# A mixture of experts on one core: gate and up products take both exact parts of the tokens as one 512-column operand, and the token search is spread one product a step over a whole expert

## The chip, the cores and the metric

The kernel runs on one core of a Trainium2 chip. The metric is the device time of one execution in microseconds (us), as the median of several runs. A profile of one further execution gives the time of every instruction on every engine: PE (TensorE matrix products), PEld (TensorE weight loads, which overlap PE), DVE (VectorE), ACT (ScalarE), POOL (GpSimd) and SP (SyncE, which issues DMAs). An instruction is named by its line in the kernel, its engine and operation, and output<-inputs by the program's names.

## The reference, cut to what matters

A layer has a mixer (normalisation, gated delta rule in two directions, pooling, output projection) and then a mixture of experts. The change touches the second half only. Of `T = 2048` tokens of width `D = 1024`, each of 16 experts takes the `cap = 256` tokens with the highest router probability.

```python
def _expert_choice_ffn(xn, router_w, w_gate, w_up, w_down):
    cap = EC_CAPACITY * T // N_EXPERTS
    probs = jax.nn.softmax(jnp.einsum('btd,de->bte', xn, router_w).astype(jnp.float32), axis=-1)
    gate, idx = lax.top_k(jnp.swapaxes(probs, 1, 2), cap)
    xg = xn[bidx, idx]
    h = jax.nn.silu(jnp.einsum('becd,edf->becf', xg, w_gate)) * jnp.einsum('becd,edf->becf', xg, w_up)
    y = jnp.einsum('becf,efd->becd', h, w_down) * gate[..., None].astype(xn.dtype)
    return jnp.zeros_like(xn).at[bidx, idx].add(y)
```

The layer's output is `h` plus this sum, normalised once more. `w_gate` and `w_up` are 1024x2048 and `w_down` 2048x1024 per expert, all float32.

## The kernel before, in words

Products are made nearly exact in float32: an operand is split into a part `hi` that the fast float32 format (fp32r) holds and the rest `lo`, and a product is the sum of `hi·hi`, `hi·lo` and `lo·hi`, three matrix products into the same PSUM tile (`split3`, L26 to L32). The stationary operand of a product is a 128x128 block that is loaded first, the moving one has 256 or 512 columns.

The expert stage (`experts`) is a loop over 16 experts, and in it over 8 chunks of 256 columns of `w_gate` and `w_up` (256 rows of `w_down`). `weights` (L1046) loads a chunk (three tiles of 1 MB by SP), ACT copies each into its `hi` part (`hg`, `hu`, `hd`, L1061) and DVE subtracts to get `lo` (`lg`, `lu`, `ld`, L1062). There are two sets of these tiles, so a chunk is prepared while the one before is used. A chunk has two blocks of 128 columns, so an expert has 16 blocks and the stage 256.

A block has three pieces on PE. Gate and up (`gate_up`, L1124): for each, 8 slices of the 1024 rows, and for each slice `split3` with the block of the weights stationary and the token parts `xh` and `xl` (256 columns each) moving, 48 products of 256 columns in all, into the two halves of one PSUM tile `pg`. Then ACT and DVE make the activation from `pg` (L1134 to L1136, the sigmoid by way of a tanh) and split it into `hh` (ACT, L1138) and `hlo` (DVE, L1139). Down (`down`, L1142): 12 products of 512 columns, with `hh` or `hlo` stationary, into four PSUM tiles `y`, which collect over the expert's 16 blocks. The down piece of a block is issued after the gate and up pieces of the next block (`behind`).

The tokens of an expert are found by `topk` (L966): ten steps, each of which compares the probabilities with eight thresholds (DVE, L984), counts (DVE, L988), adds the counts over partitions by one small product `fc` (PE, L990), and picks the next threshold (DVE, L993, L995, L981); then four small products `fr` rank the chosen tokens (L1008, L1009). Each step waits for the one before. It is run for expert 0 ahead of the loop, for expert 1 in the first chunk, and then for five, five and four experts at a time. `tokens` (L1084) turns ranks into row numbers (32 small products `pl`, L1094), `gather` (L1104) fetches the rows (POOL) and transposes them (PE, L1117; ACT and DVE make `xh` and `xl` from PSUM tile `pt`, L1119 and L1120).

What sets the order on an engine: the framework's scheduler puts the instructions of the program into one list per engine, and within a list they run in that order, each waiting for its operands. PSUM has 8 banks: two for `pg`, four for `y`, one for `pt` and one (`pl`) for the search and the row numbers.

Of the kernel before, what the change touches and what calls it, by code (L numbers as in the profile page):

```python
# [14 lines left out]
P = 128  # L15
# [19 lines left out]
class Kernel:  # L35
# [9 lines left out]
    def constants(self, c, mix):  # L45
# [20 lines left out]
        self.mhalf = c.tile([P, 8], F32, name="mhalf")  # L66
# [899 lines left out]
    def topk(self, e0, n, tk, pt, tag, tag0=None):  # L966
# [9 lines left out]
        for r in range(10):  # L976
# [12 lines left out]
            ps = pt.tile([P, n, 8], F32, name="fc", tag=tag if r else tag0 or tag)  # L989
# [29 lines left out]

        ps, rank = ranks(q)  # L1020
# [6 lines left out]
        nc.vector.tensor_tensor(sel[:, 0], rank, q[:, 0], op=OP.add)  # L1027
        _, rank = ranks(sel)
        nc.vector.tensor_tensor(rank, rank, sel[:, 0], op=OP.mult)
        slot = tk.tile([P, n, NT], F32, name="slot", bufs=2)  # L1030
        nc.vector.tensor_scalar(slot, rank, -1.0, None, op0=OP.add)
        return {e0 + k: slot[:, k] for k in range(n)}

    def expert_weights(self, ctx):
# [14 lines left out]
        def weights(e, fc, eng=nc.vector):  # L1049
            W = {}  # L1050
            for nm, w in (("g", wg), ("u", wu), ("d", wd)):
# [7 lines left out]
                o = e // 4 * 4 if nm != "d" else e % 4 * 4  # L1059
                hi, lo = (self.placed(hl, part + nm, sh, o) for part in "hl")  # L1060
# [9 lines left out]
    def experts(self, ctx, dr):  # L1070
# [8 lines left out]
        psg = E(tc.tile_pool(name="psg", bufs=2, reuse_waits="tile", space=bass.MemoryType.PSUM))  # L1079
# [4 lines left out]
        def tokens(e, slot):  # L1084

            oh = self.raw.tile([P, NT, CAP], BF, name="oh", tag="r")
            for n in range(NT):
                nc.vector.tensor_scalar(oh[:, n], self.iota, slot[:, n:n + 1], None, op0=OP.is_equal)
            c = xp.tile([P, 2, 5], F32, name="lc")
            for t in range(2):  # L1090
                ps = pst.tile([P, 5], F32, name="pl")
                for n in range(NT):
                    seg, a = divmod(n, 2)
                    nc.tensor.matmul(ps, oh[:, n, t * P:t * P + P], self.what[:, a, e, seg],  # L1094
                                     start=(n == 0), stop=(n == NT - 1))
                nc.vector.tensor_copy(c[:, t], ps)
# [5 lines left out]
            return idx, gate  # L1102

        def gather(idx, e):  # L1104
            xh, xl = (self.placed(xp, nm, [P, KD, CAP], e % 4 * 4) for nm in ("xh", "xl"))
# [6 lines left out]
            for kp in range(KD // 2):  # L1112
# [8 lines left out]
            return xh, xl  # L1121

        def gate_up(W, f, x, e):

            pg = psg.tile([P, 2, CAP], F32, name="pg")
# [7 lines left out]
            s = hp.tile([P, CAP], F32, name="s", bufs=1)  # L1133
            nc.scalar.activation(s, pg[:, 0], AF.Tanh, scale=0.5)  # L1134
            nc.vector.scalar_tensor_tensor(s, s, 1.0, pg[:, 0], op0=OP.add, op1=OP.mult)
            nc.vector.scalar_tensor_tensor(s, s, 0.5, pg[:, 1], op0=OP.mult, op1=OP.mult)  # L1136
            hh, hl_ = (self.placed(hp, nm, [P, 1, CAP], e // 4 * 4)[:, 0] for nm in ("hh", "hlo"))
# [13 lines left out]
        def scatter(ys, idx, gate):  # L1151
            for t in range(2):
                yo = yp.tile([P, D], F32, name=f"yo{t}")
# [11 lines left out]
        def norm(o, h, sq):  # L1165
# [3 lines left out]
            nc.vector.scalar_tensor_tensor(o, h, ss, tail["w"], op0=OP.mult, op1=OP.mult)  # L1169

        def tail_load(idx):
            w = xp.tile([P, D], F32, name="fnw", tag="xl")
# [3 lines left out]
            hg = xp.tile([P, 2, D], F32, name="hg", tag="xh")  # L1176
# [5 lines left out]
        def tail_rows(j):  # L1182
            h = xp.tile([P, D], F32, name="fh", tag="xg")
            nc.sync.dma_start(h, dr["h"][j * P:j * P + P, :])
            o = yp.tile([P, D], F32, name="fo", tag=f"yo{j % 2}")
            norm(o, h, o)
            nc.sync.dma_start(out2[j * P:j * P + P, :], o)

        def tail_last(ys, idx, gate):
            for t in range(2):  # L1190
                h = tail["h"][:, t]
                for n in range(2):
# [3 lines left out]
                o = yp.tile([P, D], F32, name="fo", tag=f"yo{t}")  # L1196
                norm(o, h, o)
                nc.gpsimd.indirect_dma_start(out=out2, out_offset=bass.IndirectOffsetOnAxis(ap=idx[:, t:t + 1], axis=0),  # L1198
                                             in_=o, in_offset=None)


        slots = self.topk(0, 1, tk, pst, "pl")
        nxt = tokens(0, slots.pop(0))
        xnext = gather(nxt[0], 0)
        behind = None
        for e in range(NE):
            (idx, gate), x = nxt, xnext
            ys = [psy.tile([P, 512], F32, name=f"y{n}") for n in range(4)]
            for fc in range(NF):
                W = first.pop(0) if first else weights(e, fc)  # L1210
                for f in range(FC // P):
                    h = gate_up(W, f, x, e)
                    if behind:
                        behind()
                    ft = fc * (FC // P) + f

                    def behind(e=e, W=W, f=f, h=h, ys=ys, ft=ft, idx=idx, gate=gate):
                        down(W, f, h, ys, ft == 0, ft == FF // P - 1)
                        if ft == FF // P - 1:
                            (scatter if e < NE - 1 else tail_last)(ys, idx, gate)  # L1220
# [81 lines left out]
```

## Time and profile before

| | us |
|---|---|
| median of 3 runs | 3402.22 (3400.2 to 3404.77) |
| profiled execution | 3406.23 |
| its span, first to last instruction | 3404.5 |
| PE busy | 3250.1 (95% of the span) |
| PEld busy | 2939.4 (86%) |
| DVE busy | 2155.9 (63%) |
| ACT busy | 1504.8 (44%) |

The busy time of PE counts each product until its result is written, and successive products overlap, so a busy PE is not yet a PE at its peak: what a product costs in a dense stretch is the time from its start to the next one's start. The first expert's products begin 1165 us into the span and the last ones end at about 3387 us; the clock that the chip grants to PE is full (1.0) through this stage.

### The profile page before, as it was taken

How to read it: one execution, taken by the hardware profiler on the slowest of the kernel's cores; microseconds unless marked ns; L12 is line 12 of the kernel's file. 1: busy time of each engine (PE TensorE's matmuls, PEld its weight loads, DVE VectorE, ACT ScalarE, POOL GpSimd, SP SyncE). 2: the span in 40 equal slices, each digit the busy share in tenths (PEclk: the TensorE clock that was granted, in tenths of full speed). 3: DMA queues.
4: the chain of work that ended last, by engine and by line, in shares of the span. 5: the costliest groups of instructions: out<-in, count | busy, mean ns of one | idle time of the engine just before them, and what ended most of it. 6: DMA issues, size and time to landing. Idle time of an engine off the chain costs nothing. (4 is left out here: it accounts for less than half of the span.)

```text
span 3404.5 us, 54803 instructions
## 1 busy us (share of the span) xinstructions
PE 3250.1 (95%) x21934; PEld 2939.4 (86%) x21934; DVE 2155.9 (63%) x3277; ACT 1504.8 (44%) x2426; POOL 549.3 (16%) x746
## 2 busy tenths in 40 slices
PE   8989989798999499999999999999999999999997
PEld 6877777688888399999999999999999999999997
DVE  7753878666654668665556576665656766656564
ACT  5543663455432244444444444444444444444453
POOL 3531457451121200000000000000000000000012
PEclk9999999899999699999999999999999999999999
DMA  5452444598753546656556575565665656667584
GB/s 158 116 158 84 129 136 122 186 273 265 256 191 118 198 156 210 204 178 219 198 185 211 185 223 198 178 215 182 206 203 179 212 198 186 211 186 223 198 291 148
DMA packets 514383, 644.62 MB, mean 189 GB/s; under 512 B 57168, under 2 KB 413136, under 8 KB 514128
## 3 DMA queue, kind: packets, MB, share of 16 engines
q1 hardware_dynamic: 499856, 597.60, 53.4%
q0 software_dynamic: 9664, 35.13, 4.3%
q10 hardware_dynamic: 4608, 8.39, 0.8%
q8 instruction: 172, 2.82, 0.3%
q14 instruction: 83, 0.68, 0.1%
HBM read 548.23 MB, written 92.02 MB: 188 GB/s over the span
## 5 line engine op out<-in xcount | busy, mean ns | idle before, releaser
L30 PE MATMUL pg<-xh,hg 128*128 128x256 f32 x2048 | 581.1, 284 | 2.5 <-DVE s L1136 1.6
L31 PE MATMUL pg<-xl,hg 128*128 128x256 f32 x2048 | 576.8, 282 | 0.5 <-DVE xl L1120 0.5
L30 PE MATMUL pg<-xh,hu 128*128 128x256 f32 x2048 | 576.4, 281 | 0.0
L32 PE MATMUL pg<-xh,lg 128*128 128x256 f32 x2048 | 576.0, 281 | 0.0
L32 PE MATMUL pg<-xh,lu 128*128 128x256 f32 x2048 | 575.3, 281 | 0.0
L31 PE MATMUL pg<-xl,hu 128*128 128x256 f32 x2048 | 574.2, 280 | 0.0
L1062 DVE TENSOR_TENSOR ld<-rd,hd 128x2048 fp32r<-128x2048 f32 x127 | 291.0, 2291 | 269.9 <-ACT hd L1061 269.7
L30 PEld LDWEIGHTS pg<-xh,hg 128*128 128x128 f32 x2048 | 386.0, 189 | 12.2 <-DVE s L1136 2.7
L31 PEld LDWEIGHTS pg<-xl,hg 128*128 128x128 f32 x2048 | 386.4, 189 | 10.5 <-DVE xl L1120 1.1
L32 PEld LDWEIGHTS pg<-xh,lg 128*128 128x128 f32 x2048 | 386.3, 189 | 1.7
L30 PEld LDWEIGHTS pg<-xh,hu 128*128 128x128 f32 x2048 | 385.8, 188 | 0.1
L31 PEld LDWEIGHTS pg<-xl,hu 128*128 128x128 f32 x2048 | 385.5, 188 | 0.1
L32 PEld LDWEIGHTS pg<-xh,lu 128*128 128x128 f32 x2048 | 385.4, 188 | 0.1
L1148 PE MATMUL y<-hd,hh 128*128 128x512 f32 x1024 | 326.6, 395 | 1.4 <-ACT hh L1138 1.3
L1148 PE MATMUL y<-ld,hh 128*128 128x512 f32 x1024 | 320.6, 394 | 0.0
L1148 PE MATMUL y<-hd,hlo 128*128 128x512 f32 x1024 | 319.4, 394 | 0.0
L1138 ACT CAST hh<-s 128x256 fp32r<-128x256 f32 x256 | 104.0, 406 | 486.9 <-DVE s L1136 486.9
L1062 DVE TENSOR_TENSOR lu<-ru,hu 128x2048 fp32r<-128x2048 f32 x127 | 290.9, 2290 | 42.8 <-ACT hu L1061 42.5
L1061 ACT CAST hd<-rd 128x2048 fp32r<-128x2048 f32 x128 | 243.9, 1905 | 167.4 <-PE y L1148 166.1
L1062 DVE TENSOR_TENSOR lg<-rg,hg 128x2048 fp32r<-128x2048 f32 x127 | 290.9, 2291 | 32.3 <-ACT hg L1061 32.1
L1061 ACT CAST hu<-ru 128x2048 fp32r<-128x2048 f32 x128 | 244.3, 1908 | 99.5 <-PE pg L31 95.6
L1061 ACT CAST hg<-rg 128x2048 fp32r<-128x2048 f32 x128 | 244.3, 1908 | 76.4 <-PE pg L31 72.5
(314 smaller groups left out, 5810.5 us busy)
## 6 DMA issues: line engine op xcount, KB each, us to landing
rg<-in_expert_w_gate_dram SPq DMA_DIRECT2D x128, 1024.0 KB, 6.1
ru<-in_expert_w_up_dram SPq DMA_DIRECT2D x128, 1024.0 KB, 6.1
rd<-in_expert_w_down_dram SPq DMA_DIRECT2D x128, 1024.0 KB, 5.1
wr<-in_w_in_dram SPq DMA_DIRECT2D x40, 512.0 KB, 4.1
xin<-in_x_dram SPq DMA_DIRECT2D x16, 512.0 KB, 4.4
d_P<-pp SPq DMA_DIRECT2D x32, 256.0 KB, 2.3
kT<-d_kT SPq DMA_DIRECT2D x32, 256.0 KB, 4.5
v<-d_v SPq DMA_DIRECT2D x32, 256.0 KB, 4.7
```

The lines of the kernel that those rows point to most:

```text
L30: nc.tensor.matmul(ps, lh, rh, start=first, stop=False)
L31: nc.tensor.matmul(ps, lh, rl, start=False, stop=False)
L32: nc.tensor.matmul(ps, ll, rh, start=False, stop=last)
L1061: nc.scalar.copy(hi, r)
L1062: eng.tensor_tensor(lo, r, hi.bitcast(F32), op=OP.subtract)
L1138: nc.scalar.copy(hh, s)
L1148: nc.tensor.matmul(ys[t * 2 + n], a[:, ts], b[:, f, n * 512:n * 512 + 512], start=st, stop=sp_)
```

## The change

Token parts: `gather` makes one tile `xx` with `xh` and `xl` beside each other, 512 columns per slice. For a slice of gate or up there are now two products: the weights' `hi` against all 512 columns, and the weights' `lo` against the first 256. The first half of the PSUM tile then has `hi·hi`, the second the two cross terms, so each of gate and up has a whole `pg` tile (three bufs), and ACT copies the second half out and DVE adds the first (L1143, L1144) before the activation goes on. A block's gate and up have 32 products and not 48.

Search: `topk` and `tokens` are generators now; each `next` issues the work up to the next small product. The search for expert e+2 runs alone (for experts 1 and 2 together in expert 0), one step per block. The row numbers are sought at blocks 4 and 5 (7 and 8 in expert 0), the rows fetched two blocks after, and the four groups of transposes stand in the last four blocks. Search, row numbers and transposes share one PSUM bank.

Down: for each of the four `y` tiles the three products stand together; before, two tiles took turns. The tiles `yo` and `fo` are gone, results go into `xg` buffers or stay in place, and the weights' tiles start at fixed offsets. Nothing ahead of the expert stage differs but a constant's width (`mhalf`).

```diff
-            ps = pt.tile([P, n, 8], F32, name="fc", tag=tag if r else tag0 or tag)
+            yield
+            ps = pt.tile([P, n, 8], F32, name="fc", tag=tag)
             nc.tensor.matmul(ps, self.onesb, cnt, start=True, stop=True)
...
-        psg = E(tc.tile_pool(name="psg", bufs=2, reuse_waits="tile", space=bass.MemoryType.PSUM))
+        psg = E(tc.tile_pool(name="psg", bufs=3, reuse_waits="tile", space=bass.MemoryType.PSUM))
...
-            c = xp.tile([P, 2, 5], F32, name="lc")
+            yield
+            ps = pst.tile([P, 2, 5], F32, name="pl", tag="pt")
             for t in range(2):
-                ps = pst.tile([P, 5], F32, name="pl")
                 for n in range(NT):
                     seg, a = divmod(n, 2)
-                    nc.tensor.matmul(ps, oh[:, n, t * P:t * P + P], self.what[:, a, e, seg],
+                    nc.tensor.matmul(ps[:, t], oh[:, n, t * P:t * P + P], self.what[:, a, e, seg],
                                      start=(n == 0), stop=(n == NT - 1))
-                nc.vector.tensor_copy(c[:, t], ps)
+            c = xp.tile([P, 2, 5], F32, name="lc")
+            nc.vector.tensor_copy(c, ps)
...
-                oh = xh[:, kp * 2:kp * 2 + 2]
+                oh = xx[:, kp * 2:kp * 2 + 2, 0]
                 nc.scalar.copy(oh, pt)
-                nc.vector.tensor_tensor(xl[:, kp * 2:kp * 2 + 2], pt, oh.bitcast(F32), op=OP.subtract)
+                nc.vector.tensor_tensor(xx[:, kp * 2:kp * 2 + 2, 1], pt, oh.bitcast(F32), op=OP.subtract)
...
-            for half, nm in ((0, "g"), (1, "u")):
+            a = []
+            for nm in ("g", "u"):
                 hi, lo = W[nm]
+                pg = psg.tile([P, 2, CAP], F32, name="pg")
                 for k in range(KD):
-                    split3(nc, pg[:, half], (hi[:, k, fs], lo[:, k, fs]), (x[0][:, k], x[1][:, k]),
-                           k == 0, k == KD - 1)
+                    nc.tensor.matmul(pg, hi[:, k, fs], x[:, k], start=k == 0, stop=False)
+                    nc.tensor.matmul(pg[:, 1], lo[:, k, fs], x[:, k, 0], start=False, stop=k == KD - 1)
+                r = hp.tile([P, CAP], F32, name="r" + nm)
+                nc.scalar.copy(r, pg[:, 1])
+                nc.vector.tensor_tensor(r, pg[:, 0], r, op=OP.add)
+                a.append(r)
...
-                for a, b, st, sp_ in ((h[0], hi, first, False), (h[0], lo, False, False), (h[1], hi, False, last)):
-                    for n in range(2):
+                for n in range(2):
+                    for a, b, st, sp_ in ((h[0], hi, first, False), (h[0], lo, False, False), (h[1], hi, False, last)):
                         nc.tensor.matmul(ys[t * 2 + n], a[:, ts], b[:, f, n * 512:n * 512 + 512],
                                          start=st, stop=sp_)
...
+            if e == 0:
+                search, pace, choose = self.topk(1, 2, tk, pst, "pt", slots), 2, 7
+            else:
+                search, pace, choose = (self.topk(e + 2, 1, tk, pst, "pt", slots) if e + 2 < NE else iter(())), 1, 4
+            listing = iter(())
+            for ft in range(FF // P):
...
+                if ft == choose and e + 1 < NE:
+                    listing = tokens(e + 1, slots.pop(e + 1))
+                h = gate_up(W, f, x)
+                if behind:
+                    behind()
+                for _ in range(pace):
+                    next(search, None)
+                next(listing, None)
+                if e + 1 < NE:
+                    if ft == choose + 2:
+                        xnext, turn = gather(found[e + 1][0])
+                    if ft > last - KD // 2:
+                        turn(ft - last - 1 + KD // 2)
```

How the lists change, first on PE around the start of a down piece in the middle of the stage (`y` tiles by their numbers, `hd` and `ld` the weights' parts, `hh` and `hlo` the stationary ones). Before:

```order
L30 MATMUL pg<-xh,hu 128x256
L31 MATMUL pg<-xl,hu 128x256
L32 MATMUL pg<-xh,lu 128x256
L1148 MATMUL y_15481<-hd,hh 128x512
L1148 MATMUL y_15482<-hd,hh 128x512
L1148 MATMUL y_15481<-ld,hh 128x512
L1148 MATMUL y_15482<-ld,hh 128x512
L1148 MATMUL y_15481<-hd,hlo 128x512
L1148 MATMUL y_15482<-hd,hlo 128x512
```

And now, at the start of another down piece:

```order
L1140 MATMUL pg<-xx,hg 128x512
L1141 MATMUL pg<-xx,lg 128x256
L1163 MATMUL y_17899<-hd,hh 128x512
L991 LDWEIGHTS onesb
L991 MATMUL fc<-fcnt,onesb 128x8
L1163 MATMUL y_17899<-ld,hh 128x512
L1163 MATMUL y_17899<-hd,hlo 128x512
L1163 MATMUL y_17900<-hd,hh 128x512
L1163 MATMUL y_17900<-ld,hh 128x512
L1163 MATMUL y_17900<-hd,hlo 128x512
```

Three products of a slice have become two, the three products of a `y` tile stand together, and a product of a search (`fc`) stands among them. In this row the down piece starts within a gate piece: the scheduler has let the gate piece of a later block begin first.

On DVE, one chunk in the middle of the stage (`ld`, `lg`, `lu` are the splits of the weights, `s` the activation). Before:

```order
L1062 TENSOR_TENSOR ld<-rd,hd 128x2048
L1062 TENSOR_TENSOR lg<-rg,hg 128x2048
L1062 TENSOR_TENSOR lu<-ru,hu 128x2048
L1135 SCALAR_TENSOR_TENSOR s<-s,pg 128x256
L1136 SCALAR_TENSOR_TENSOR s<-s,pg 128x256
L1139 TENSOR_TENSOR hlo<-s,hh 128x256
```

And now, with the adds (`rg`, `ru`) and a step of a search among them:

```order
L994 SCALAR_TENSOR_TENSOR ftot<-fc,fth 128x8
L996 TENSOR_REDUCE fbase<-ftot 128x1
L981 TENSOR_TENSOR fth<-bits,fbase 128x8
L1064 TENSOR_TENSOR ld<-rd,hd 128x2048
L984 TENSOR_TENSOR fge<-fpr,fth 128x128
L1149 SCALAR_TENSOR_TENSOR s<-s,rg 128x256
L1064 TENSOR_TENSOR lu<-ru,hu 128x2048
L1144 TENSOR_TENSOR ru<-pg,ru 128x256
L988 TENSOR_REDUCE fcnt<-fge 128x8
L1150 SCALAR_TENSOR_TENSOR s<-s,ru 128x256
L1144 TENSOR_TENSOR rg<-pg,rg 128x256
L1154 TENSOR_TENSOR hlo<-s,hh 128x256
```

Between a block's second add and its `hlo` there now stand a count of the search and the next block's first add.

## Rows read from the trace of the kernel before

**Rows 1.** The page: busy us, share of the span and instructions of each engine.

```profile
PE 3250.1 (95%) x21934; PEld 2939.4 (86%) x21934; DVE 2155.9 (63%) x3277; ACT 1504.8 (44%) x2426; POOL 549.3 (16%) x746
```

**Rows 2.** Waits on PE from 1190 us: waiting <- waited for: us, times, longest.

```profile
PE pg L30 <- DVE s L1136: 1.6, 2, 1.4
PE y L1148 <- ACT hh L1138: 1.3, 1, 1.3
PE pt L1117 <- DVE xl L1120: 1.0, 1, 1.0
PE pg L31 <- DVE xl L1120: 0.5, 2, 0.3
PE fc L990 <- DVE fcnt L988: 0.2, 1, 0.2
```

**Rows 3.** By window, `pg` alone: length, PE busy (products), granted clock, DMA share, GB/s.

```profile
1455.83:1461.43 5.60, 5.60 (x48) 1.00 0.59 91
1946.14:1951.80 5.66, 5.66 (x48) 1.00 1.06 381
3209.27:3215.08 5.81, 5.81 (x48) 1.00 1.02 362
1500.00:2500.00 1000.00, 685.20 (x5559) 1.00 0.61 197
```

**Rows 4.** The same, products of 512 columns: `y`, then `mm`, then `po`.

```profile
1951.80:1954.58 2.78, 2.78 (x12) 1.00 0.41 129
1500.00:2500.00 1000.00, 342.60 (x1392) 1.00 0.61 197
...
230.39:304.75 74.36, 74.36 (x329) 1.00 0.37 111
...
1081.53:1092.49 10.96, 10.96 (x48) 1.00 0.24 96
```

**Rows 5.** Timeline, PE: start, duration, line, out<-in, count; a search product.

```profile
2007.74 0.39 PE L1148 MATMUL y<-hd,hlo 128*128 128x512 f32 x1
2007.98 0.19 PE L990 MATMUL fc<-fcnt,onesb 128*128 128x40 bf16 x1
2008.01 0.48 PE L1148 MATMUL y<-hd,hlo 128*128 128x512 f32 x1
```

**Rows 6.** Groups of DVE instructions from 1180 us: count, busy us, mean ns, idle before.

```profile
L1139 DVE TENSOR_TENSOR hlo<-s,hh 128x256 fp32r<-128x256 f32 x256 | 108.5, 424 | 93.6 <-ACT hh L1138 92.1
...
L988 DVE TENSOR_REDUCE fcnt<-fge 128x40 bf16<-128x640 bf16 x20 | 16.3, 814 | 0.2
L984 DVE TENSOR_TENSOR fge<-fpr,fth 128x640 bf16<-128x640 f32 x18 | 14.8, 824 | 0.5
...
L984 DVE TENSOR_TENSOR fge<-fpr,fth 128x128 bf16<-128x128 f32 x9 | 2.6, 289 | 0.2
L988 DVE TENSOR_REDUCE fcnt<-fge 128x8 bf16<-128x128 bf16 x9 | 2.5, 281 | 0.1
...
L981 DVE TENSOR_TENSOR fth<-bits,fbase 128x8 int32<-128x8 int32 x9 | 1.5, 164 | 0.2
```

**Rows 7.** Busy time by window: DVE alone, then ACT alone.

```profile
1500.00:2500.00 1000.00, 620.04 (x805) 1.00 0.61 197
...
1500.00:2500.00 1000.00, 431.69 (x434) 1.00 0.61 197
```

**Rows 8.** Timeline of one block: DVE, and the down piece on PE.

```profile
1945.39 2.29 DVE L1062 TENSOR_TENSOR lu<-ru,hu 128x2048 fp32r<-128x2048 f32 x1 [0.49 <-ACT hu L1061]
1947.60 0.41 DVE L1135 SCALAR_TENSOR_TENSOR s<-s,pg 128x256 f32<-128x256 f32 x1
1948.94 0.42 DVE L1139 TENSOR_TENSOR hlo<-s,hh 128x256 fp32r<-128x256 f32 x1 [0.47 <-ACT hh L1138]
...
1952.73 0.62 PE L1148 MATMUL y<-hd,hlo 128*128 128x512 f32 x2
```

**Rows 9.** Timeline, PE: the row numbers of expert 0.

```profile
1150.68 0.57 PE L1094 MATMUL pl<-what,oh 128*128 128x5 bf16 x16 [0.26 <-DVE lc L1096]
```

More of the change, by code (lines that the diff above doesn't have):

```diff
@@ L1027, in topk @@
         nc.vector.tensor_tensor(sel[:, 0], rank, q[:, 0], op=OP.add)
+        yield
         _, rank = ranks(sel)
         nc.vector.tensor_tensor(rank, rank, sel[:, 0], op=OP.mult)
-        slot = tk.tile([P, n, NT], F32, name="slot", bufs=2)
+        slot = tk.tile([P, n, NT], F32, name="slot", bufs=3)
         nc.vector.tensor_scalar(slot, rank, -1.0, None, op0=OP.add)
-        return {e0 + k: slot[:, k] for k in range(n)}
+        slots.update({e0 + k: slot[:, k] for k in range(n)})
     def expert_weights(self, ctx):
@@ L1058, in weights @@
                 nc.sync.dma_start(r, src)
-                o = e // 4 * 4 if nm != "d" else e % 4 * 4
-                hi, lo = (self.placed(hl, part + nm, sh, o) for part in "hl")
+                hi, lo = (placed(hl, part + nm, sh, 4 if nm == "d" else 0) for part in "hl")
                 nc.scalar.copy(hi, r)
@@ L1101, in tokens, with gather @@
             nc.vector.tensor_tensor(gate, gate, c[:, :, 4], op=OP.add)
-            return idx, gate
-        def gather(idx, e):
-            xh, xl = (self.placed(xp, nm, [P, KD, CAP], e % 4 * 4) for nm in ("xh", "xl"))
+            found[e] = idx, gate
+        def gather(idx):
+            xx = self.placed(xp, "xx", [P, KD, 2 * CAP], 4).rearrange("p k (s c) -> p k s c", s=2)
             xg = []
@@ L1111, in gather, with turn @@
                 xg.append(g)
-            for kp in range(KD // 2):
+            def turn(kp):
                 pt = pst.tile([P, 2, CAP], F32, name="pt")
@@ L1152, in scatter @@
             for t in range(2):
-                yo = yp.tile([P, D], F32, name=f"yo{t}")
+                yo = xp.tile([P, D], F32, name="yo", tag="xg")
                 for n in range(2):
@@ L1163, in experts, with norm @@
         tail = {}
-        def norm(o, h, sq):
+        def norm(h):
+            sq = yp.tile([P, D], F32, name="sq")
             ss = xp.tile([P, 1], F32, name="fss")
@@ L1205, in experts, with run @@
-        behind = None
+                                             in_=h, in_offset=None)
+        slots, found = {}, {}
+        def run(gen):
+            for _ in gen:
+                pass
+        run(self.topk(0, 1, tk, pst, "pt", slots))
+        run(tokens(0, slots.pop(0)))
+        xnext, turn = gather(found[0][0])
+        for kp in range(KD // 2):
+            turn(kp)
+        behind, last = None, FF // P - 1
         for e in range(NE):
-            (idx, gate), x = nxt, xnext
+            (idx, gate), x = found.pop(e), xnext
@@ L1208, in experts @@
             ys = [psy.tile([P, 512], F32, name=f"y{n}") for n in range(4)]
[L1209 to L1220, printed above, removed]
+            if e == 0:
+                search, pace, choose = self.topk(1, 2, tk, pst, "pt", slots), 2, 7
+            else:
+                search, pace, choose = (self.topk(e + 2, 1, tk, pst, "pt", slots) if e + 2 < NE else iter(())), 1, 4
@@ new lines, in experts, with behind @@
+            listing = iter(())
+            for ft in range(FF // P):
+                fc, f = divmod(ft, FC // P)
+                if f == 0:
+                    W = first.pop(0) if first else weights(e, fc)
+                if ft == choose and e + 1 < NE:
[11 more added lines that the diff above has]
+                        turn(ft - last - 1 + KD // 2)
+                def behind(e=e, W=W, f=f, h=h, ys=ys, ft=ft, idx=idx, gate=gate):
+                    down(W, f, h, ys, ft == 0, ft == last)
+                    if ft == last:
+                        (scatter if e < NE - 1 else tail_last)(ys, idx, gate)
@@ L1221, in experts @@
                 if e == NE - 1:
[L1222 removed]
+                    if ft == 1:
                         tail_load(idx)
[L1224 to L1234 removed]
+                    if ft % 2:
+                        for j in range(ft - 1, ft + 1):
+                            tail_rows(j)
```

51 lines of the change are left out of this document (17 added, 34 removed).

## The prediction

> **What bounds the kernel now.** I read the shares of the engines first [rows 1]: PE is busy for 95% of the span, DVE for 63%. That alone doesn't say that PE sets the time, so I read next what PE waited for once the expert stage runs [rows 2]: the five kinds of wait come to 4.6 us in a stage of some 2220 us. Third, the count of products in dense windows [rows 3, 4]: from 1500 to 2500 us there were 5559 products of 256 columns and 1392 of 512. The window 1946.14 to 1951.80 holds exactly the 48 gate and up products of a block, start to start: 5.66 / 48 = 117.9 ns each. The 12 down products behind it take 2.78 / 12 = 231.7 ns each. With these, 5559 x 0.1179 + 1392 x 0.2317 = 978 of the 1000 us; transposes, row numbers and search fill the rest. So the stage is one dense stream of products, at the higher clock level, 2.4 GHz (granted 1.00 in every window), and its length is the sum of the products' spacings. What makes another engine busier costs nothing unless PE comes to wait for it.
>
> **The change part by part.**
>
> *Gate and up.* Columns are the same: three products of 256 become one of 512 and one of 256. What can be saved is the part of a product's time that doesn't grow with its columns. From the two spacings, 2 x 117.9 - 231.7 = 4.1 ns. For each of 16 experts x 16 blocks x 2 x 8 slices = 4096 slices one product goes, so 4096 x 4.1 ns = 16.8 us less. The bounds: the spacings differ from place to place. A block at 1455.83 has 5.60 / 48 = 116.7 ns, one at 3209.27 has 121.0 [rows 3]. A 512-column product takes 226.7 ns in the densest stretch (the mm products from 230.39 us: 329 counted, the first of which began before the window, so 74.36 / 328) and 233.2 in the slowest (the po products, 10.96 / 47) [rows 4]. A slice, now 3 x 117.9 = 353.7 ns, would be 343.4 by the lowest pair and 354.2 by the highest: from 42 us less to 2 us more. I take 16.8, since the two spacings that I use stand one behind the other in this stage, and near the middle.
>
> The Trainium skill, on the page "TensorE: Matmul & The Clock Gate", section "Back-to-back issue gap", gives N/2.4 + 2.5 ns for the spacing of N columns, so a product less would be worth 2.5 ns, 10.2 us in all. The trace disagrees with the formula on both sizes: 109.2 and 215.8 ns by it, 117.9 and 231.7 measured, and the excess grows with the columns.
>
> *Down.* The 3072 products stay; three in a row now go into the same PSUM tile, where two tiles took turns. The mm and po products also went three in a row into one tile, at 226.7 and 233.2 ns; so per product between 5.0 less and 1.5 more, -15 to +5 us in all. I take 0, between them.
>
> *Search.* Before, four searches ran inside the loop (one expert, then five, five and four); now 14 (one pair and 13 singles). A search has 14 small products, so 56 become 196. One of them stands between two down products that start at 2007.74 and 2008.01, 0.27 us apart where 0.2317 is the rule, so it costs 0.038 us [rows 5]. 140 x 0.038 = 5.3 us more. From fc's own start to the next one's it is 0.03, by which it would be 4.2.
>
> *Evacuation.* Each of 512 pieces gets an ACT copy and a DVE add of 256 columns. The nearest DVE row, hlo, takes 0.424 us [rows 6], so 217 us more on DVE; on ACT about as much. A search step for one expert has two longer DVE operations (0.289 and 0.281) and three short ones like L981 (0.164), 1.06 us; for five, 0.824 and 0.814 and three of some 0.2, 2.24 us [rows 6]. 130 single steps and ten of the pair (about 1.4) make 152 us, against 10 x 1.06 + 20 x 2.24 + ten for four experts at some 1.9, 74: 78 us more. DVE is busy for 620 us of 1000 in the stage now [rows 7]; 217 + 78 = 295 over some 2220 us add 133, so about 75%. ACT goes from 43% to 53%. Neither becomes the bound by its sum.
>
> Is anything late? The path from the end of the up piece to hlo has five instructions before (tanh, two products with s, cast, subtraction) and five now (copy, add, one product with s, cast, subtraction): gate's half can go ahead while up runs. So its length stays, and what grows is the queue in front of it on DVE. In the block shown [rows 8] the split lu kept DVE until 1947.68, hlo was done at 1949.36 and PE read it at 1952.73: 3.37 us to spare with a whole split in the way. The new neighbours, two adds and a search step, are 0.85 + 1.06 = 1.9 us. The spare time covers that, and the order now puts a gate piece of a later block ahead of some down pieces, which gives more. I take no new wait. If the cover is gone, PE waits at the down piece and everything behind it with it; that is a rival below. The bounds here are the 4.6 us of waits that could vanish [rows 2] and that rival's price.
>
> *One bank for search, row numbers and transposes; the ends.* A transpose or a search product now waits until DVE has emptied the bank for the one before. The nearest row is the wait of transposes for xl, 1.0 us in the whole stage [rows 2]; a block gives every such step 8 us, and I take 0. At the start, the second half of expert 0's row numbers waited 0.26 us for the first copy [rows 9]; both halves now have room, -0.3. The four removed DVE or PSUM tiles and the fixed offsets have no instruction. Weight loads by SP and POOL's fetches are the same ones, and the fetch of the rows comes earlier in an expert than before.
>
> Sum: -16.8 + 5.3 - 0.3 = -11.8 us. The profiled execution took 3406.2 us (its span is 3404.5), so 3394.4 in its terms. It was 4.0 us above the median of the runs, 3402.2; in their terms 3390.
>
> **The rivals.**
>
> *Columns alone set the time.* If the two spacings that I took apart are both only columns (2 x 116.7 - 233.2 = 0.2 ns of fixed part, with the lowest of the one and the highest of the other, [rows 3, 4]), nothing is saved and the 5.3 us of the search remain: 3407. For it: the spacing varies by more than the 4.1 ns on which my gain rests. Against it: the same stage, one block behind the other, gives 4.1. By the Trainium skill's 2.5 ns (above) it would be -10.2 + 5.3 - 0.3, so 3397.
>
> *DVE comes late for the down piece* (the other side). In each chunk three splits of 2.29 us stand on DVE; where two of them, a search step and the adds fall between up's end and hlo, 4.6 + 1.1 + 0.8 = 6.5 us stand in the way, against the 5.7 us (one split and the 3.37 us to spare) that the block shown could bear [rows 8]. PE would wait 0.8 us there. In every second of the 128 chunks, my estimate, that is 51 us, and 3402 - 12 + 51 = 3441. It decides from 11.8 / 64 = 0.18 us per such chunk. For it: DVE at 75%, in a fixed order with a step that waits for PE in each block. Against it: the weights' splits are done a chunk ahead, and PE waited for hh once in 256 blocks [rows 2].
>
> *The wide products run as in the first stage.* If the 4096 and the 3072 products of 512 columns take the mm's 226.7 ns, a slice costs 226.7 + 117.9 = 344.6, 9.1 less, 37 us in all, and down gains 15: -52 + 5, 3355. For it: mm also puts three into one tile in turn. Against it: so does po, at 233.2.
>
> *The shared bank makes PE wait.* An expert has 14 search products, row numbers and four groups of transposes through one bank; if the 1.0 us wait [rows 2] came once per expert, +15 us: 3405. Against it: a block's length lies between the steps.
>
> **How the numbers follow.** Forecast 0.50; columns alone 0.17; DVE late 0.15; wide products fast 0.12; shared bank 0.06. The forecast's own range is 3378 to 3402 (half the spread of the slice's price, and the vanishing waits). A measurement of this kernel can tell about 0.2%, 6.8 us, from no change: faster is below 3395.4, slower above 3409. Faster: 0.46 of the forecast's 0.50 and the 0.12; same: 0.04 of the forecast, 0.13 of columns alone, 0.05 of the bank; slower: 0.15, 0.04 and 0.01 of these. The range 3370 to 3422 leaves out most of the fast and of the late case, about 0.2 together.
>
> **What would show it.** In the profile after: 4096 products pg<-xx,hg and hu of 512 columns and 4096 of 256, in dense windows (512 + 256) some 350 ns a pair; if it is 354, columns alone were right, if 344, the fast case. DVE at about 75% in the middle of the stage and ACT at 53%; waits on PE still below some 10 us, with no group of waits for hh, hlo or s; if they reach tens of us, DVE was late. Search products 196 in the loop, each moving the next by 0.04 us. The prediction is wrong if the stage's end moves by more than the products' spacings say.

## The result: slower by 1.0%, and where the time went

| | before | after |
|---|---|---|
| median of the runs, us | 3403.49 (4 runs) | 3436.86 (3433.11 to 3438.86, 4 runs) |
| ratio, 95% interval | | 1.0098 [1.008, 1.0115] |
| span of the profiled execution, us | 3404.5 | 3437.1 |
| first `pg` to last `y` product, us | 2221.5 | 2255.1 |

The forecast was 3390 us. All of the loss lies in the expert stage. The page's shares after, to be read against [rows 1]:

```profile
PE 3256.4 (95%) x17978; PEld 2747.0 (80%) x17978; DVE 2366.7 (69%) x4443; ACT 1660.4 (48%) x2938; POOL 603.4 (18%) x746
```

Almost a fifth of the products is gone and PE's share is the same. What PE waited for from 1170 us on (waiting <- waited for: us, times, longest) says more; [rows 2] came to 4.6 us, these to 30.1:

```profile
PE pt L1123 <- DVE xx L1126: 13.3, 13, 1.1
PE pg L1140 <- DVE ru L1144: 5.6, 2, 4.0
PE y L1163 <- ACT hh L1153: 4.7, 2, 4.1
PE pg L1141 <- DVE lg L1064: 2.3, 1, 2.3
PE fr L1009 <- DVE fq L1029: 1.9, 1, 1.9
PE pl L1097 <- DVE oh L1091: 1.5, 1, 1.5
PE fr L1009 <- DVE fq L1003: 0.8, 1, 0.8
```

To share out the 33.6 us I added up, in both traces, the distance from each product's start to the next one's; of a distance over 60 ns longer than is usual (the median) for its kind, the excess is kept apart (it holds waits, half-clock stretches and short hiccups of some 85 ns):

| us | before | after | |
|---|---|---|---|
| gate and up | 1449.3 | 1433.2 | -16.1 |
| down | 712.3 | 708.5 | -3.8 |
| search `fc`, `fr` | 2.3 | 7.2 | +4.9 |
| row numbers, transposes | 35.1 | 35.0 | 0 |
| excess | 22.6 | 71.1 | +48.5 |

By usual distances the products became 15 us shorter, which looks like the forecast, but part of that came back as short hiccups: of the 48.5 us more of excess 11 are hiccups. In places over 0.15 us the excess went from 7.5 to 44.8, and 43.1 of that stands in four places:

*13 expert boundaries, 17.4 us.* DVE, then PE, at one of them (timeline: start, duration, line, out<-in, idle before and what ended it):

```profile
1452.19 2.28 DVE L1064 TENSOR_TENSOR lu<-ru,hu 128x2048 fp32r<-128x2048 f32 x1
1454.39 0.28 DVE L1091 TENSOR_SCALAR oh<-iota,slot 128x256 bf16<-128x256 bf16 x1
1454.58 0.42 DVE L1144 TENSOR_TENSOR ru<-pg,ru 128x256 f32<-128x256 f32 x1
1454.92 1.85 DVE L1091 TENSOR_SCALAR oh<-iota,slot 128x256 bf16<-128x256 bf16 x9
1456.68 0.42 DVE L1149 SCALAR_TENSOR_TENSOR s<-s,rg 128x256 f32<-128x256 f32 x1
1457.01 0.69 DVE L1126 TENSOR_TENSOR xx<-pt,xx 128x512 fp32r<-128x512 f32 x1
...
1453.15 0.60 PE L1123 MATMUL pt<-ident,xg 128*128 128x128 f32 x4
...
1456.45 0.28 PE L1141 MATMUL pg<-xx,lg 128*128 128x256 f32 x1
1457.75 0.66 PE L1123 MATMUL pt<-ident,xg 128*128 128x128 f32 x4 [1.03 <-DVE xx L1126]
```

ACT had copied the transposes of 1453.15 by 1454.37, but ten row comparisons (`oh`, for the expert after), an addition and a step of the activation stood ahead of `xx` in DVE's list. The last transposes need the same bank, so PE stands until `xx` has been made.

*Expert 0, 11.5 us.* The search of experts 1 and 2 ends, and its last products and the row numbers follow each other on PE without gate and up products between them:

```profile
1236.40 0.19 PE L1009 MATMUL fr<-fq,onesb 128*128 128x64 bf16 x1 [0.81 <-DVE fq L1003]
1238.51 0.19 PE L1009 MATMUL fr<-fq,onesb 128*128 128x32 bf16 x1 [1.90 <-DVE fq L1029]
1240.26 3.55 PE L1097 MATMUL pl<-what,oh 128*128 128x5 bf16 x32 [1.53 <-DVE oh L1091]
1246.74 0.58 PE L1141 MATMUL pg<-xx,lg 128*128 128x256 f32 x1 [2.30 <-DVE lg L1064]
```

*3158 us, 5.8,* where DVE stood 8.60 us before it wrote a row number (`idx`), until a scatter (`d_h<-yo,idx`) had ended:

```profile
3161.29 0.16 DVE L1102 SCALAR_TENSOR_TENSOR idx<-lc 128x2 int32<-128x2 f32 x1 [8.60 <-DMA d_h<-yo,idx]
...
3162.68 0.79 PE L1163 MATMUL y<-hd,hh 128*128 128x512 f32 x1 [4.14 <-ACT hh L1153]
```

*The last expert, 8.4,* with the waits for the addition `ru` above. Then, the granted clock around the stall of expert 0 (length, busy of PE, PEld, DVE, ACT and POOL, clock, DMA share, GB/s):

```profile
1235.00:1240.80 5.80, 1.52 (x11) 0.74 (x9) 4.34 (x27) 3.89 (x3) 0.00 (x0) 1.00 0.00 0
1241.00:1251.00 10.00, 7.59 (x44) 5.57 (x44) 9.22 (x18) 0.00 (x0) 4.45 (x2) 0.50 0.61 200
1251.30:1256.00 4.70, 4.70 (x28) 4.18 (x27) 4.46 (x3) 2.18 (x2) 0.00 (x0) 1.00 1.05 393
```

PE was busy for 1.52 of 5.80 us, and then had 0.50, the lower level of 1.2 GHz, for about 10 us.

### The profile page after: what moved, and what is told of

Read it like the earlier page. It is cut to its first block, busy times and chain, and to the rows that moved or that the text cites. A ratio compares the mean times of both kernels' runs of the same rounds, so it can differ in the third digit from the quotient of the medians.

```text
span 3437.1 us, 48517 instructions
## 1 busy us (share of the span) xinstructions
PE 3256.4 (95%) x17978; PEld 2747.0 (80%) x17978; DVE 2366.7 (69%) x4443; ACT 1660.4 (48%) x2938; POOL 603.4 (18%) x746
## 5 line engine op out<-in xcount | busy, mean ns | idle before, releaser
L1140 PE MATMUL pg<-xx,hg 128*128 128x512 f32 x2048 | 749.5, 400 | 5.6 <-DVE ru L1144 5.6
L1140 PE MATMUL pg<-xx,hu 128*128 128x512 f32 x2048 | 738.6, 396 | 0.1
L1141 PE MATMUL pg<-xx,lg 128*128 128x256 f32 x2048 | 579.6, 283 | 2.3 <-DVE lg L1064 2.3
L1141 PE MATMUL pg<-xx,lu 128*128 128x256 f32 x2048 | 579.7, 283 | 0.0
L1140 PEld LDWEIGHTS pg<-xx,hg 128*128 128x128 f32 x2048 | 387.8, 189 | 94.1 <-DVE ru L1144 9.1
L1140 PEld LDWEIGHTS pg<-xx,hu 128*128 128x128 f32 x2048 | 385.4, 188 | 89.8 <-issue 5.0
L1141 PEld LDWEIGHTS pg<-xx,lg 128*128 128x128 f32 x2048 | 388.7, 190 | 12.1 <-DVE lg L1064 2.8
L1141 PEld LDWEIGHTS pg<-xx,lu 128*128 128x128 f32 x2048 | 386.1, 189 | 2.0
L30 PE MATMUL mm<-xh,wh 128*128 128x512 f32 x640 | 255.8, 400 | 8.3 <-DVE th L310 4.2
L1143 ACT COPY rg<-pg 128x256 f32<-128x256 f32 x256 | 94.4, 369 | 342.0 <-PE pg L1141 337.7
L31 PE MATMUL mm<-xl,wh 128*128 128x512 f32 x640 | 254.5, 398 | 0.1
```

The costliest lines, as they stand in the source:

```text
L30: nc.tensor.matmul(ps, lh, rh, start=first, stop=False)
L31: nc.tensor.matmul(ps, lh, rl, start=False, stop=False)
L1140: nc.tensor.matmul(pg, hi[:, k, fs], x[:, k], start=k == 0, stop=False)
L1141: nc.tensor.matmul(pg[:, 1], lo[:, k, fs], x[:, k, 0], start=False, stop=k == KD - 1)
L1143: nc.scalar.copy(r, pg[:, 1])
```

## The experiments

All are edits of the changed kernel, except one of the kernel before. Each edit makes the scheduler write all lists anew, so a run shows its edit and what the scheduler made of it. In the diffs "..." stands for lines left out. Times are medians; the ratio is to the kernel before, run beside it. The theories by their letters: P, the new places of search, row numbers and transposes; D, and sharper V, DVE late with what PE needs; B, the shared bank; W, it takes the wide products themselves; K, the two banks of a wide pair; T, the place of the transposes.

### The two parts alone, one bank, and the additions

`wide_old_search`: search, row numbers and transposes back at their old places and in two banks; two banks for `pg`.

```diff
-        psg = E(tc.tile_pool(name="psg", bufs=3, reuse_waits="tile", space=bass.MemoryType.PSUM))
+        psg = E(tc.tile_pool(name="psg", bufs=2, reuse_waits="tile", space=bass.MemoryType.PSUM))
...
-            ps = pst.tile([P, 2, 5], F32, name="pl", tag="pt")
+            ps = pst.tile([P, 2, 5], F32, name="pl")
...
+                    if fc == 6:
+                        xnext = all_turns(found[e + 1][0])
```

> The wide gate and up products alone: search in batches of five, row numbers and all four transpose groups at the places they have in the kernel before, with a bank of their own for the transposes and two banks for gate and up. Theory P (the loss comes from where the search, the row numbers and the transposes now stand in the engines' order, and the wide products gain what was forecast): 3403 - 20 for the products = 3384 us (3378 to 3392), waits of TensorE in the expert stage back under 25 us from 71. Rival D (the loss comes from VectorE, which has two more additions per chunk and is late with what TensorE needs): at least 30 of the 48 us of new waits stay, 3414 to 3435 us.

3425.5, 1.0064 [1.0047, 1.008]. P's time fails and D's holds: this kernel loses 21 us without the new search. But the transposes wait for `xx` no longer between 1300 and 3200 us; what PE waits for there is a `pg` bank, of which this run has two and not three, so it doesn't tell what the wide products lose with three:

```profile
PE pg L1140 <- DVE rg L1144: 7.7, 10, 3.3
PE pg L1140 <- DVE ru L1144: 1.6, 1, 1.6
```

`narrow_new_search`:

```diff
-                    nc.tensor.matmul(pg, hi[:, k, fs], x[:, k], start=k == 0, stop=False)
-                    nc.tensor.matmul(pg[:, 1], lo[:, k, fs], x[:, k, 0], start=False, stop=k == KD - 1)
+                    split3(nc, pg[:, half], (hi[:, k, fs], lo[:, k, fs]), (x[:, k, 0], x[:, k, 1]),
+                           k == 0, k == KD - 1)
...
```

> The other part alone: gate and up go back to six 256-column products a pair and to the evacuation of before, search, row numbers and transposes stay spread out and share one bank. Theory P: 3403 + 5 for the small products + most of the 48 us of waits = 3435 to 3460 us, with waits at each expert boundary for the split of the transposes. Rival D: 3409 us (3404 to 3414), no waits at the boundaries.

3408.9, 1.0016 [1.0006, 1.0026], no waits at the boundaries, as D said. It keeps the stall of expert 0, which is 8.8 us of excess here, so it is chance that the whole difference comes near the 5.3 us at which I priced the search.

`own_bank` (the searches take the bank `pl` too):

```diff
-        psg = E(tc.tile_pool(name="psg", bufs=3, reuse_waits="tile", space=bass.MemoryType.PSUM))
+        psg = E(tc.tile_pool(name="psg", bufs=2, reuse_waits="tile", space=bass.MemoryType.PSUM))
...
-            ps = pst.tile([P, 2, 5], F32, name="pl", tag="pt")
+            ps = pst.tile([P, 2, 5], F32, name="pl")
...
```

> The changed kernel with a bank of their own for the transposes; search and row numbers have another, and gate and up are left with two banks. Rival B (it is the shared bank that makes TensorE wait): the 13 us of waits of the transposes and 15 to 25 us in all go, 3412 to 3422 us. Theory P: the transposes have one bank as before and wait for the split of the group ahead, which stands behind the row comparisons on VectorE, so most of it stays, 3430 to 3440 us.

3446.0, 1.0122 [1.0105, 1.0138]. Between 1300 and 3200 us the waits of transposes for `xx` are gone, but the two banks left for `pg` bring others:

```profile
PE pg L1140 <- DVE ru L1144: 19.0, 16, 2.0
PE pg L1140 <- DVE rg L1144: 3.1, 13, 0.5
```

So B isn't refuted by this run; the bank that it gives to one is taken from the other.

`no_adds`:

```diff
-                nc.vector.tensor_tensor(r, pg[:, 0], r, op=OP.add)
```

> The changed kernel without the 512 additions of the two halves of a gate or up sum; it leaves out the larger half of the sum, so what comes out is another number. VectorE has 512 x 0.4 = 205 us less work, the products are the same. Rival D: most of the 48 us of new waits go, 3390 to 3400 us. Theory P: the waits belong to places where VectorE has row comparisons, splits or the last expert's norm ahead of what TensorE needs, they shrink by less than half: 3418 to 3437 us.

3404.5, 1.0001 [0.9991, 1.001]: 32 us less, and no wait on PE from 1300 to 3200 us. D seems right. But the edit takes away two things, work on DVE and DVE's part in emptying the bank.

`narrow_adds` puts the additions on the narrow products:

```diff
+                nc.scalar.activation(r, pg[:, half], AF.Copy, scale=0.5)
+                nc.vector.scalar_tensor_tensor(r, pg[:, half], 0.5, r, op0=OP.mult, op1=OP.add)
...
```

> The 256-column products with the spread search (3409 us) and, added, the evacuation of the wide products: a ScalarE copy and a VectorE addition of 0.4 us for each gate and each up sum (half the sum plus half the sum, so the value is the same). Theory V: the 512 additions alone bring waits, at the expert boundaries and in the last expert, 3409 + 15 to 35 = 3424 to 3444 us. Rival W (the wide products themselves leave VectorE too little time, the additions alone are hidden): 3405 to 3414 us.

3411.7, 1.0021 [1.001, 1.0032]: 2.8 us over `narrow_new_search`. V fails as I put it: the same 512 additions cost next to nothing here and 32 us with wide products. At the boundary shown above the comparisons stood ahead of `xx` here too:

```profile
1452.63 1.65 DVE L1091 TENSOR_SCALAR oh<-iota,slot 128x256 bf16<-128x256 bf16 x8
1454.19 0.69 DVE L1126 TENSOR_TENSOR xx<-pt,xx 128x512 fp32r<-128x512 f32 x1
...
1450.23 0.60 PE L1123 MATMUL pt<-ident,xg 128*128 128x128 f32 x4
1450.58 0.36 PE L30 MATMUL pg<-xx,hg 128*128 128x256 f32 x1
```

but behind the last transposes the list had 79 gate and up products in a row, 9.2 us of work, where the changed kernel has 12. That suggested the banks (K): a wide pair needs two. `narrow_adds_split` gives the narrow products two as well:

```diff
+                pg = psg.tile([P, 2, CAP], F32, name="pg")
+                pgs.append(pg)
...
```

> The 256-column products with the additions (3412 us with one bank for a pair), and now gate and up in a bank each, as the wide ones have them. Theory K (the banks: a pair holds two of the three, so TensorE runs out of products to do while it waits for a transpose or an evacuation): 3412 + 12 to 30 = 3424 to 3442 us. Rival W (it needs the wide products themselves): 3408 to 3416 us.

3413.4, 1.0029 [1.0018, 1.0039]. So K fails as a reason for the boundary waits.

What differs in the lists is how far apart the last two of the four groups of transposes start. In the changed kernel it is 4.3 to 4.6 us (some 3.5 without the wait) at the 13 boundaries that wait, and 11.6 and 31.1 at the two that don't; in `narrow_new_search`, `narrow_adds`, `narrow_adds_split` and `no_adds`, which wait at none, it is 8.8 us or more at every boundary. This is read from the lists; no edit tried it by itself.

### Taking work off DVE

`oh_pool`:

```diff
-                nc.vector.tensor_scalar(oh[:, n], self.iota, slot[:, n:n + 1], None, op0=OP.is_equal)
+                (nc.vector if e < 1 else nc.gpsimd).tensor_scalar(oh[:, n], self.iota, slot[:, n:n + 1], None, op0=OP.is_equal)
```

> The changed kernel with the 15 x 16 row comparisons of experts 1 to 15 on GpSimd in place of VectorE. Theory V (VectorE works its list off in order and is late with what TensorE needs; at each expert boundary 16 comparisons of 0.2 us stand between the splits of the transposes): the 13 waits of 1.19 us and the small ones after them go, 3437 - 18 = 3419 us (3412 to 3424). Rival B (the one bank shared by search, row numbers and transposes makes the wait, whatever VectorE does): 3432 to 3442 us with the boundary waits still there.

3437.8, 1.0091 [1.0074, 1.0108]. The boundary waits are gone, as V said, and the time is the same: from 1300 to 3200 us PE now waits elsewhere (in a profiled execution of 3452.2 us, above the median), and one comparison takes 1.35 us on POOL, where DVE took 0.28. At five boundaries the last two groups start 3.2 us apart and no transpose waits (the five waits stand some 10 us later), so closeness without the comparisons on DVE doesn't bring the boundary waits:

```profile
PE pg L1140 <- DVE rg L1144: 13.1, 5, 2.6
...
L1091 POOL TENSOR_SCALAR oh<-iota,slot 128x256 bf16<-128x256 bf16 x224 | 300.0, 1354 | 997.7 <-DVE lg L1064 945.0 <-DVE ld L1064 52.7
```

`ld_pool`, and the same edit in the kernel before, `before_ld_pool`:

```diff
-                eng.tensor_tensor(lo, r, hi.bitcast(F32), op=OP.subtract)
+                (nc.gpsimd if nm == "d" else eng).tensor_tensor(lo, r, hi.bitcast(F32), op=OP.subtract)
```

> The changed kernel with one of the three splits of a weight chunk (the down weight's) on GpSimd, which takes 4.5 us for it where VectorE takes 2.29. VectorE is relieved of 126 x 2.29 = 289 us, more than the additions put on it. Theory V: as without the additions, the boundary waits and those of the last expert go, 3437 - 30 = 3407 us (3400 to 3414). Rival (the two engines slow each other, or the later split makes the down products wait): 3425 us or more, with a split on VectorE over 2.5 us or waits of the down products.

> The kernel before with the same split on GpSimd. Theory V: before had nothing to win from a relieved VectorE, its waits are 22 us of which some 15 belong to the start and the last expert: 3400 us (3394 to 3406). Rival (relieving VectorE gains in any kernel, so that ld_pool says nothing about the change): 3390 us or less.

3465.7, 1.0179 [1.0162, 1.0196], and 3452.5, 1.0138 [1.0121, 1.0155]. V fails in both, and so does the rival of `before_ld_pool`; the rival of `ld_pool` holds, the two engines slow each other, as the last section shows. With expert 1 searched early as well and the third buffer it was 3464.7.

`act_both`:

```diff
...
-                nc.scalar.copy(r, pg[:, 1])
-                nc.vector.tensor_tensor(r, pg[:, 0], r, op=OP.add)
+                nc.scalar.copy(r, pg)
+                nc.vector.tensor_tensor(r[:, 0], r[:, 0], r[:, 1], op=OP.add)
```

> The changed kernel with both halves of a gate or up sum copied out by ScalarE, so that the bank is free without VectorE; the addition then reads SBUF. VectorE has the same number of instructions, ScalarE 512 x 0.2 = 100 us more. Theory K: the waits for a bank (5.6 us for the up additions, those in the last expert) go, and those for the transposes stay: 3424 to 3432 us. Rival V (VectorE's load, wherever it is read from): 3434 to 3442 us.

3426.7, 1.0061 [1.0043, 1.008]: 10 us less, in K's range but not by its reason. The waits for a `pg` bank went, and as much waiting for `hh` came in the last expert, where the excess only fell from 8.4 to 7.9 us; of the 9.2 us of excess that went, 5.8 are the wait at 3158 us, which these lists don't have. The boundary waits stay, now on the products behind the transposes, which read `xx`. In both kernels a late `xx` ends them, there by way of the transposes' bank, here as an operand:

```profile
PE pg L1140 <- DVE xx L1126: 12.6, 13, 1.0
PE y L1163 <- ACT hh L1153: 6.4, 6, 1.8
```

### Moving what stands at the four places

`search01`:

```diff
-        run(self.topk(0, 1, tk, pst, "pt", slots))
+        run(self.topk(0, 2, tk, pst, "pt", slots))
...
-            if e == 0:
-                search, pace, choose = self.topk(1, 2, tk, pst, "pt", slots), 2, 7
...
```

> The changed kernel with expert 1 searched together with expert 0 ahead of the experts, so that expert 0 has the one-product pace of the others and no stall of its own. Theory V: the 11 us of waits at 1235 to 1251 us and the half clock behind them (about 5 us) go, and the search of two experts ahead costs 1 to 2 us more at the start: 3422 us (3418 to 3428). Rival (the stall moves to the next place where VectorE is behind): 3432 us or more.

3426.6, 1.0066 [1.0049, 1.0083]: the stall of expert 0 is gone, worth 10 us.

`tail_pool`:

```diff
+            if rows:
+                nc.scalar.activation(h, h, AF.Copy, scale=ss)
+                nc.gpsimd.tensor_tensor(h, h, tail["w"], op=OP.mult)
+                return
```

and `bufs=3` for `idx` and `gate`.

> The changed kernel with the last expert's 16 row norms taken off VectorE (ScalarE scales, GpSimd multiplies) and a third buffer for row numbers and gates. Theory V: the wait of 4.3 us at 3158 us and those of 1.8, 0.8 and 4.2 us in the last expert go with the half clock behind them: 3437 - 14 = 3423 us (3419 to 3430). Rival (the last expert is bound by ScalarE, which gets 16 x 1.1 us more): 3435 us or more.

3441.8, 1.0119 [1.0102, 1.0136]. In its trace the last `y` product starts 5.4 us earlier, but what follows takes 25.4 us and not 18.2: POOL's last norms are late. The three edits (`oh_pool`, `search01`, `tail_pool`) together gave 3440.4 and not the hoped 3390.

`early_turns`:

```diff
-                    if ft > last - KD // 2:
-                        turn(ft - last - 1 + KD // 2)
+                    if choose + 3 < ft < choose + 4 + KD // 2:
+                        turn(ft - choose - 4)
```

> The changed kernel with the four transpose groups of the next expert four steps (34 us) earlier, so that none is left at the expert boundary. Theory T (the 13 waits of 1.19 us come from the last transposes standing at the boundary): they go, 3437 - 17 = 3420 us (3414 to 3426). Rival (VectorE's lateness shows elsewhere in the expert): 3432 us or more.

3415.4, 1.0039 [1.0024, 1.0053]: 21.5 us less, with DVE's work unchanged, and no wait on PE from 1300 to 3200 us. This is T, in its range; 17.4 us is what the boundaries had cost, and the wait at 3158 us went with them.

`early_search01`: the edits of `search01` and `early_turns` and the third buffer for `idx` and `gate`, together:

> The earlier transposes, expert 1 searched ahead of the experts, and a third buffer for row numbers and gates, together. Theory T: 3437 - 17 - 10 - 6 = 3404 us (3398 to 3410), no better than the kernel before, since the waits of the last expert (some 10 us with the clock) stay. Rival: 3418 us or more.

3402.6, 0.9996 [0.9987, 1.0006]: the whole loss is undone, and the edits add up (21.5 + 10.3, and 2.4 more). What PE still waits for, from 1170 to 3400 us:

```profile
PE pg L1140 <- DVE ru L1144: 6.3, 3, 4.1
PE y L1163 <- ACT hh L1153: 0.3, 1, 0.3
```

`early_search01_narrow` has the 256-column products in this kernel, with the diff of `narrow_new_search`:

> early_search01 (3402.6 us) with the six 256-column products a pair and the evacuation of the kernel before. Theory T (with the transposes out of the boundary the wide products give what their count says): 3403 + 12 to 22 = 3415 to 3425 us. Rival (the narrow kernel had its waits at the first search, not at the boundary, and loses them too: 3409 - 8 = 3401 us; the wide products then gain nothing net): 3397 to 3406 us.

3401.9, 0.9989 [0.998, 0.9998]. The rival: with the boundary waits out of the way the wide products are worth nothing that the time shows. PE is busy throughout in both, the wide one first (window of steady experts, columns as above):

```profile
1800.00:2900.00 1100.00, 1100.00 (x6098) 930.22 (x6097) 800.31 (x1587) 549.94 (x731) 63.83 (x32) 1.00 0.62 199
```

```profile
1800.00:2900.00 1100.00, 1100.00 (x8113) 1019.16 (x8113) 742.57 (x1326) 471.85 (x475) 45.94 (x32) 1.00 0.62 199
```

`early_search01_act` adds the edit of `act_both`:

> early_search01 with both halves of a sum copied out by ScalarE. If the waits left in the last expert (1.3, 1.3 and 4.2 us for the addition of the up sum) are for the bank: 3403 - 7 = 3396 us (3391 to 3400), faster than the kernel before. If they are for VectorE's order, whoever empties the bank: 3400 to 3406 us.

3403.0, 0.9992 [0.9983, 1.0001]. The waits of the last expert move from the bank to `hh` (7.1 us in 6) and stay. No version beat the kernel before by what can be told from no change.

## Why the prediction was wrong, step by step

*The step that failed is "I take no new wait".* I measured the spare time, 3.37 us, at one block in the middle of an expert [rows 8], found that 1.9 us of new neighbours fit, and let that stand for 256 blocks. Between 1300 and 3200 us PE waited at no such block: it waited at the boundaries and once at 3158 us. The lists around the boundaries, expert 0 and the last expert are made differently from a typical block's, and I had looked at none of them.

*That one bank would cost 0 failed at the same place.* Transposes did wait for the bank, 13 times 1.0 us, as the shared-bank rival put it "once per expert", at +15 us against 17.4 measured. It was given 0.06. Its reason was wrong: search and row numbers weren't in the way, the wait is for `xx` of the group ahead; and in `act_both`, where no transpose waits for the bank, PE waited for the last `xx` itself. I set the rival aside because "a block's length lies between the steps"; that is so in the code's order, while the scheduler put the last three groups within 12 us. The sign stood in the kernel before: the 1.0 us of [rows 2] that I took as the nearest row was this very wait, at its first boundary, where the last two groups start 2.7 us apart (about 8 at the others):

```profile
1308.98 0.66 PE L1117 MATMUL pt<-ident,xg 128*128 128x128 f32 x4 [1.01 <-DVE xl L1120]
```

*DVE late* (0.15, 3441 us) named the engine, but not the place: of the 30.1 us only 4.7 were at down pieces, where it had 51. That its time is nearly right is luck. The load was well foreseen: DVE 75% and ACT 53% forecast, 72% and 50% found, against [rows 7]:

```profile
1500.00:2500.00 1000.00, 992.67 (x5505) 836.89 (x5506) 722.02 (x1423) 497.50 (x658) 68.37 (x30) 1.00 0.61 196
```

Load wasn't enough to forecast waits: at unchanged load `early_turns` was 21.5 us shorter, and the additions, costly with wide products, cost 2.8 us with narrow ones.

*Gate and up, -16.8 us.* By usual distances it was -16.1, but that sum can't show the gain: in `narrow_new_search`, whose gate and up products are those of the kernel before, it is 1431.7, 17.6 less than before. With the short hiccups the changed kernel has 1455.0 against 1463.2, 8.2 us less, and a pair (512 + 256) is 355 ns on average. Over experts 4 to 11, gate and up took 91.51 us an expert before, 90.85 in `early_search01` and 91.44 in its narrow twin: 0.66 and 0.59, so 10.6 and 9.4 us over 16 experts. New lists alone move this sum too: it is 91.01 to 91.27 in the three narrow kernels with the late transposes, and 90.77 to 90.92 in three wide ones that don't wait there either (`early_turns`, `no_adds`, `early_search01_act`), so all that can be said is a gain of some 1 to 11 us. Two unbroken gate and up pieces in the changed kernel took as long as the 48 products of 5.66 us in [rows 3], where 350 ns a pair would make 5.60; the median of its 18 such pieces is 5.65, and so is that of 140 before:

```profile
1744.69:1750.35 5.66, 5.66 (x33) 1.00 0.41 52
1884.40:1890.05 5.65, 5.65 (x33) 1.00 0.42 57
```

So *columns alone* was nearer than it looked: the 4.1 ns is the difference of two spacings in one block, of which at best 2.6 are left over whole experts, and in `early_search01` the waits of the last expert (6.6 us on PE against 2.0 in the twin), which differ from list to list, take part of the rest. The term was mis-sized as well, though that alone would have left the time within the stated range. *Wide products fast* found nothing for it. The formula that the prediction took from the Trainium skill, on the page "TensorE: Matmul & The Clock Gate", section "Back-to-back issue gap", is given there for a single product by itself and not for a dense stream.

*Search, +5.3:* +4.9 measured. *Down, 0:* -3.8 by usual distances and -0.4 with the hiccups, within its bounds.

Three things stay open. Neither DVE's load nor the number of banks a pair holds explains alone why the additions hurt in the changed kernel and not in the narrow ones; the lists differ in how close the last two groups of transposes stand, but why the scheduler wrote them so stays unknown. What cleared the wait at 3158 us in `early_search01` was not tried apart: `early_turns`, `act_both` and `tail_pool` alone have none there either. And the waits of the last expert were moved but not removed.

## What to carry to other kernels

Before pricing a change of the products, go to the seams (first pass, boundary between passes, last pass) and look there at what the other engines have in line ahead of what the bound engine needs; a block from the middle doesn't tell. A gain that is a difference of two spacings read in one block is to be checked against sums over a long stretch, hiccups included, and against a kernel that has new lists but not the gain. And when waits come from the order, move the waited-for work earlier before shifting load to GpSimd: the first gave 21.5 us here, the second nothing or a loss.

## What the runs showed of the hardware that I had not expected

*POOL was no spare room for DVE here.* With one split on POOL, the splits that stay on DVE get longer. Two rows of `ld_pool`, POOL then DVE:

```profile
1955.54 4.63 POOL L1064 TENSOR_TENSOR ld<-rd,hd 128x2048 fp32r<-128x2048 f32 x1 [3.70 <-ACT hd L1063]
...
1957.30 5.02 DVE L1064 TENSOR_TENSOR lg<-rg,hg 128x2048 fp32r<-128x2048 f32 x1 [2.54 <-ACT hg L1063]
```

POOL ends at 1960.17, DVE at 1962.32, 2.15 us later, about one split's own length (2.29), as if DVE stood until POOL was done. From 1500 to 2500 us `lg` took 4.35 us on average and 2.29 in the changed kernel:

```profile
L1064 DVE TENSOR_TENSOR lg<-rg,hg 128x2048 fp32r<-128x2048 f32 x57 | 248.1, 4353 | 157.4 <-ACT hg L1063 156.7
```

```profile
L1064 DVE TENSOR_TENSOR lg<-rg,hg 128x2048 fp32r<-128x2048 f32 x58 | 132.7, 2288 | 21.8 <-ACT hg L1063 21.8
```

Of the `lg` that began in that stretch of `ld_pool`, the 42 that overlap a split on POOL took 5.02 us on average, the 14 others 2.29. So of the 2.29 us that went to POOL 2.06 came back. The Trainium skill says why, on the page "SBUF — State Buffer", section "SBUF: two separate sides": DVE and GpSimd share a port pair as an exclusive lock, held for a whole instruction, and a DVE operation with two inputs from SBUF needs it against a GpSimd operation that reads SBUF. The trace agrees: the additions `rg`, which read one input from PSUM, took 0.41 us where they overlap a split on POOL (7 of them) and where they don't. A step of the activation with both inputs in SBUF took 4.65 us where it overlaps (7) and 0.41 elsewhere, so its average rose (first `ld_pool`, then the changed kernel):

```profile
L1149 DVE SCALAR_TENSOR_TENSOR s<-s,rg 128x256 f32<-128x256 f32 x114 | 76.9, 674 | 5.1 <-ACT s L1148 5.1
```

```profile
L1149 DVE SCALAR_TENSOR_TENSOR s<-s,rg 128x256 f32<-128x256 f32 x114 | 48.1, 422 | 3.7 <-ACT s L1148 3.3
```

In all, DVE was busy for 763 of the 1000 us from 1500 to 2500 in `ld_pool`, against 722 in the changed kernel, which has all three splits on DVE. In `before_ld_pool` `lg` took 4.10 us on average over the run; through which waits its 48 us came stays open.
